# RWKV-7 stretches of a hybrid block: one DMA queue and the prices in a written-out order

## The chip, the cores and the metric

The kernel runs on one core of one Trainium2 chip. The metric is the device time of one execution in microseconds (us). The kernel before took 2974.73 us, the median of 3 runs (2971.03 to 2976.58).

The engines are called by their short names: PE (TensorE, matmuls), PEld (its weight loads), DVE (VectorE), ACT (ScalarE), POOL (GpSimd) and SP (SyncE, which only issues DMAs). Each has its own stream of instructions, laid down when the kernel is built; a DMA is issued by an instruction in the stream of SP or ACT, with its waits.

## The reference

Two layers over 256 context tokens and 256 latent tokens of width 1024, batch 1. Each layer normalises and modulates its input, projects it, runs three mixers in both directions over the sequence, merges them by gates, and ends in a SwiGLU block:

```
for layer in range(2):
    h   = modulate(rms_norm(x), ...)              # 1024 x 512 tokens
    p   = h @ w_in                                # all mixers' inputs and the merge gates
    ml  = chunkwise mLSTM(p)                      # 4 heads of 256
    lru = depthwise conv + RG-LRU(p)
    rw  = RWKV-7(p)                               # 16 heads of 64
    y   = sum_b sigmoid(g_b) * (b @ out_b);  x += gate * (y @ w_out)
    x  += gate * swiglu(modulate(rms_norm(x), ...))
```

RWKV-7 is the recurrence that the change is about. For each head and direction, with a 64 x 64 state S:

```
S_t = S_{t-1} (diag(w_t) - kap_t^T (a_t * kap_t)) + v_t^T k_t
y_t = S_t r_t
```

The latent tokens start from the final state of the context tokens. In the last layer the outputs for context tokens aren't needed. Everything is 32-bit: each large product is split into three passes (high by low, high by high, low by high) to keep its accuracy.

## The kernel before

**Layout.** Features lie on the 128 partitions, tokens on the free axis (T = 512: context 0 to 255, latent 256 to 511). A large product is one block of 128 output features: 8 blocks of the contraction x 3 passes = 24 matmuls of 512 columns (or of 256, where only latent tokens count) into one PSUM tile `mm`. Its weights are one DMA of 512 KB into a tile `wraw` (two buffers, line 390); in two halves ACT rounds them to `whi` and DVE takes the rest as `wlo` (lines 470 and 473).

**RWKV-7 in units.** The recurrence is computed in chunks of 32 tokens. A unit u (0 to 7) is four heads and one half of the tokens: even units context, odd ones latent. Each unit passes through:

- `rw_load` (line 929): loads of the projected k, r, v and of the decay weights (`ax`), issued by SP.
- `rw_prep` (line 662): decays, normalised keys, scaled rows, then the small matmuls whose masked results are `Am` (line 781). One generator goes through the eight units in order; the preparation of unit u also waits for the chain of unit u - 3.
- `rw_solve` (line 950): the triangular system of each chunk. SP writes the blocks of `Am` to DRAM (`sc1`), loads them transposed as `N` (line 957), POOL eliminates in 30 steps of two operations on i x w elements with w = 31 - i (lines 963 and 965) and sets the diagonal (line 967), SP stores N (line 970) and loads it back into `Am` (line 975).
- `rw_tok` (line 853): token-major copies of keys and values (`UV`, `bkT`).
- `rw_chain` (line 979): eight chunks one after the other, each with some five groups of small matmuls and the steps `xs` (line 1034, DVE), `UV` (lines 1061 and 1064, ACT and DVE) and the new state `Sn` (line 1081, DVE) between them.
- `rw_tail`: norm, gate and store.

**The order.** Inside a stretch the instructions of PE, SP, DVE, ACT and POOL are laid down in an order that `weave` (line 299) works out when the kernel is built. Every task is a generator: it emits instructions and says what they cost in planned ns (`took`, `at`, `op`) or what it waits for (`until`, `wait`). `weave` keeps a planned clock `now`; of the tasks that are ready it takes the first of a fixed list: low-rank inputs, loads, preparation, chains, gate, and last the large products (`fill`). The products come earlier than their place in the list by one rule (line 332): if the columns that planned matmuls put through PE in the last `TICK` = 3413 ns of planned time are fewer than `COLS[l]`, the products get the turn. They also run whenever nothing else is ready. `TICK` appears a second time: at the end of each such tick `slow` becomes 2.0 when the tick's columns were 3100 (`THR`) or fewer, and all planned PE times are doubled until the next tick (lines 322 to 324, 350).

**The products of a stretch** (`products`, line 460): 74 blocks, first the RWKV inputs for the four pairs of units, then mLSTM's and the LRU's, whose results go to DRAM (`mld`, `lrd`). The load for product n + 2 is issued in the middle of product n (line 500), always by SP.

**Waits of the plan**: `DMW` ahead of the load of N, `DML` behind it and again behind the store of N, `DMR` behind the load back into `Am`.

**After the stretch** come the mLSTM and LRU stage, the 24 merge-gate blocks (`mg`, with `wblk`, `wload`, `wraw`: lines 411 to 417; matmuls at line 425, casts at lines 382 and 383, stores at line 1289), the merge itself and the feed-forward block. These are outside the written-out order: the framework places them, also between a stretch's instructions where they fit. In layer 1 they have 256 columns.

Of the kernel before, what the change touches and what calls it, by code (L numbers as in the profile page):

```python
# [30 lines left out]
NCH = T // CH  # L31
DSC = math.exp(-0.5)
TICK = 3413.0
DML = 4000
COLS = [4800, 4800]
GDP = 1
ORD = [0, 0]
SL = 1000
SW = 230
THR = 3100  # L40
PW = 1700
HYS = 0
DMW = 4000
DMR = 5000
JW = 4
JD = 6
# [166 lines left out]
class KB:  # L213
# [85 lines left out]
    def weave(self, tasks, cols):  # L299

        live = [[g, 0.0, None, False, 0.0, None] for g in tasks]
        fill = live[-1]
        self.now, recent = 0.0, []
        self.free = {"V": 0.0, "S": 0.0, "G": 0.0}
        tick, slow, count, burst = TICK, 1.0, 0.0, False


        def can(c):
            return c is None or (c[1] not in self.locks if c[0] == "lock" else c in self.done)

        eng = mybir.EngineType
        with self.tc.manual_schedule(engines={eng.PE, eng.SP, eng.DVE, eng.Activation, eng.Pool}):
            i = None
            while live:
                if i is None:
                    ok = [x for x in live if can(x[2])]
                    ready = [x for x in ok if x[1] <= self.now]
                    if not ready:
                        self.now = min(x[1] for x in ok)
                        continue  # L320
                    i = ready[0]
                    while self.now > tick:
                        tick += TICK
                        slow, count = (1.0 if count > THR else 2.0), 0.0
                    while recent and recent[0][0] < self.now - TICK:
                        recent.pop(0)
                    light = [x for x in ready if x[3]]
                    if light:
                        i = light[0]
                    elif fill in ready:  # L330

                        if sum(c for _, c in recent) < cols + (HYS if burst else -HYS):
                            i = fill
                        burst = i is fill
                    i[3] = False
                    if i[2] and i[2][0] == "lock":
                        self.locks.add(i[2][1])
                        i[4] = self.now
                    elif i[2]:
                        i[4] = max(i[4], self.now)  # L340
                    i[2] = None
                self.since, self.by, i[5] = i[4], i[5], None
                try:
                    k, *v = next(i[0])
                except StopIteration:
                    live.remove(i)
                    i = None
                    continue
                if k == "pe":
                    self.now += v[0] * slow  # L350
                    count += v[1]
                    recent.append((self.now, v[1]))
                    i[4] = self.now + PED
                    if i is fill:
                        i = None
                    continue
                if k == "spawn":
                    live.insert(live.index(i) + 1, [v[0], 0.0, None, False, max(self.now, self.since), None])
                    continue
                if k == "aside":  # L360
                    live.insert(0, [v[0], 0.0, None, True, v[1], None])
                    continue
                if k == "wait":
                    i[1] = i[4] = max(self.now, self.since) + v[0]
                elif k == "at":
                    i[1] = i[4] = v[0]
                elif k == "on":

                    i[1], i[3] = v[0], True
                    i[4], i[5] = v[1:] if len(v) > 1 else (v[0], None)  # L370
                elif k == "lock":
                    i[2] = (k, v[0])
                else:
                    i[2] = v[0]
                i = None
# [18 lines left out]
        self.nraw = -1  # L394
        es.callback(lambda: setattr(self, "wx", None))

    def wraw(self, src, n=1024):
        raw = self.rawtile()
        self.nc.sync.dma_start(out=raw[:, 0:n], in_=src)
        return raw  # L400

    def wpart(self, raw, i, n=512, pool=None):
# [57 lines left out]
    def products(self, jobs, h):  # L460


        raw = [self.wraw(self.A["wA"][j[0]]) for j in jobs[:2]]
        w = {}
        self.stores = []

        def part(n, i, first=False):
            hi, lo = (self.pw.tile([128, 512], F32R, name=x, tag=x, bufs=3) for x in ("whi", "wlo"))
            x = raw[n][:, 512 * i:512 * i + 512]
            self.nc.scalar.copy(hi, x)  # L470
            if not first:
                yield self.at("S", 615)
            self.nc.vector.tensor_tensor(out=lo, in0=x, in1=hi.bitcast(F32), op=ALU.subtract)  # L473
            w[2 * n + i] = [x.rearrange("p (k c) -> p k c", c=128) for x in (hi, lo)]
            yield self.end("V", 760)
            self.done.add(("w", w_id, 2 * n + i))

        def evac(n, ps):
            store = yield from jobs[n][2](ps)
            if store:  # L480
                self.stores.append(store)
            self.done.add(("evac", w_id, n))

        w_id = len(self.done)
        for i in range(2):
            yield ("aside", part(0, i, True), 0.0)
        for n, (_, t0, take) in enumerate(jobs):
            if n > 1:
                yield ("until", ("evac", w_id, n - 2))
            ps = self.mm()  # L490
            for k in range(KC):
                if k % 4 == 0:
                    yield ("until", ("w", w_id, 2 * n + k // 4))
                for i, (x, y) in enumerate(((0, 1), (0, 0), (1, 0))):
                    self.mmul(ps[:, t0:], w[2 * n + k // 4][x][:, k % 4], h[y][:, k, t0:], start=k == 0 and i == 0, stop=k == KC - 1 and i == 2)
                    yield self.took(0.0)
                if k % 4 == 0 and n + 1 < len(jobs):
                    yield ("aside", part(n + 1, k // 4), 0.0)
                    if k == 4 and n + 2 < len(jobs):
                        raw.append(self.wraw(self.A["wA"][jobs[n + 2][0]]))  # L500
                if k == 3:
                    while self.stores:
                        self.stores.pop(0)()
            yield ("aside", evac(n, ps), self.now + PED)
        yield ("until", ("evac", w_id, len(jobs) - 1))
        while self.stores:
            self.stores.pop(0)()
# [442 lines left out]
    def rw_solve(self, l, u, Am, sc1):  # L950

        nc, G, re = self.nc, self.nc.gpsimd, self.re
        if u:
            yield ("until", ("solve", l, u - 1))
        yield ("wait", DMW)
        N = re.tile([64, 32, 32], F32, name="N")
        nc.sync.dma_start(out=N, in_=sc1.rearrange("x h q s t -> (x h q) s t"))
        yield ("wait", DML)
        et = re.tile([64, 256], F32, name="et")
        for i in range(1, 31):  # L960
            w = 31 - i
            tv = et[:, 0:i * w].rearrange("p (a b) -> p a b", b=w)
            G.tensor_tensor(out=tv, in0=N[:, 0:i, i:i + 1].broadcast_to([64, i, w]), in1=N[:, i:i + 1, i + 1:32].broadcast_to([64, i, w]), op=ALU.mult)  # L963
            yield ("on", self.op("G", 240 + 2.0 * i * w) - 1500)
            G.tensor_tensor(out=N[:, 0:i, i + 1:32], in0=N[:, 0:i, i + 1:32], in1=tv, op=ALU.subtract)  # L965
            yield ("on", self.op("G", 300 + 1.85 * i * w) - 1500)
        G.memset(N.rearrange("p s t -> p (s t)")[:, 0:1024:33], -1.0)
        yield ("on", self.op("G", 100) + LAT)
        sc2 = self.dr.tile([2, 2, 16, 32, 32], F32, name="sc2")
        nc.sync.dma_start(out=sc2.rearrange("x h q s t -> (x h q) s t"), in_=N)  # L970
        yield ("wait", DML)
        for hd in range(2):
            for j in range(2):
                b = 64 * hd + 32 - 32 * j
                nc.sync.dma_start(out=Am[b:b + 32, j, :, :, 0:32].rearrange("p d c t -> p (d c) t"), in_=sc2[hd, j].rearrange("q s t -> s q t"))
        self.ready[u] = max(self.now, self.since) + DMR
        self.done.add(("solve", l, u))
# [880 lines left out]
```

## Time and profile before

| | |
|---|---|
| median of 3 runs | 2974.73 us |
| the profiled execution | 2970.17 us |
| its span, first to last instruction | 2968.5 us |
| mean granted clock of PE | 0.955 |
| PE busy | 2648.7 us, 89% |
| PEld busy | 2039.5 us, 69% |
| DVE busy | 1761.2 us, 59% |
| ACT busy | 1264.0 us, 43% |
| POOL busy | 810.0 us, 27% |
| DMA | 421.04 MB, mean 142 GB/s |

PE's busy time is an upper estimate, since matmuls overlap and their ends are modelled. The granted clock is a share of full speed: the records know 1.00 (2.4 GHz) and 0.50 (1.2 GHz), and a mean between is a mix of the two. The stretch of layer 0 lies at about 50 to 850 us, that of layer 1 at about 1700 to 2500 us. "Idle before" a group is time in which its engine did nothing, put down to what ended the wait; on an engine that nobody waits for it costs nothing.

### The profile page before, as it was taken

Reading aid. Unit: us, or ns where it says so; the run is one execution under the profiler, and the core shown is the slowest. Engines: PE = TensorE matmul, PEld = TensorE weight load, DVE = VectorE, ACT = ScalarE, POOL = GpSimd, SP = SyncE. Lnnn points to the kernel's source line nnn. Section 1 sums busy time; section 2 is a strip of 40 time slices with the busy share of each in tenths; the row PEclk is TensorE's granted clock in tenths of the full one; section 3 lists DMA queues with packets and bytes.
Section 4 is the critical chain, followed back from the end, with each engine's and each line's share of the span. In section 5 each row is a group of like instructions: output and inputs, shape, how many; then the busy total and the mean of one; then the engine's idle time right before and its main releaser. Section 6 shows DMA issues by size and latency. Waiting matters only on the chain. (4 is left out here: it accounts for less than half of the span.)

```text
span 2968.5 us, 71161 instructions
## 1 busy us (share of the span) xinstructions
PE 2648.7 (89%) x29512; PEld 2039.5 (69%) x29512; DVE 1761.2 (59%) x3642; ACT 1264.0 (43%) x2495; POOL 810.0 (27%) x1231
## 2 busy tenths in 40 slices
PE   7998999999789999999999989899996765769998
PEld 4775666666555576777777878776775654349898
DVE  5575667666468844553333456667675646767664
ACT  4443433333247732342222455444443422755553
POOL 1045545455403100010000101564645550100000
PEclk9999999999899999999999999999997886879999
DMA  6443333433254277655554445444443333327454
GB/s 225 164 143 108 115 116 112 116 113 103 62 193 126 92 234 237 216 172 167 168 166 132 126 149 163 141 130 122 132 122 93 88 101 117 93 86 255 150 183 143
DMA packets 242307, 421.04 MB, mean 142 GB/s; under 512 B 86048, under 2 KB 133408, under 8 KB 241984
## 3 DMA queue, kind: packets, MB, share of 16 engines
q1 hardware_dynamic: 240688, 415.39, 45.2%
q8 instruction: 231, 3.78, 0.5%
q10 hardware_dynamic: 1296, 1.10, 0.1%
q14 instruction: 92, 0.75, 0.1%
HBM read 348.75 MB, written 66.62 MB: 140 GB/s over the span
## 5 line engine op out<-in xcount | busy, mean ns | idle before, releaser
L259 PE MATMUL mm<-hl,whi 128*128 128x512 f32 (+1 forms) x1184 | 451.4, 381 | 9.0 <-DVE stage L549 4.7
L259 PE MATMUL mm<-hh,wlo 128*128 128x512 f32 (+1 forms) x1184 | 451.5, 381 | 0.8 <-DVE wlo L473 0.8
L259 PE MATMUL mm<-hh,whi 128*128 128x512 f32 (+1 forms) x1184 | 450.2, 380 | 0.0
L383 DVE TENSOR_TENSOR wlo<-wraw,whi 128x512 fp32r<-128x512 f32 (+1 forms) x310 | 219.3, 709 | 292.7 <-ACT whi L382 289.5
L425 PE MATMUL mm<-hl,whi 128*128 128x512 f32 (+1 forms) x1056 | 372.4, 353 | 2.5 <-ACT fg L1763 1.9
L425 PE MATMUL mm<-hh,wlo 128*128 128x512 f32 (+1 forms) x1056 | 366.8, 348 | 4.5 <-DVE wlo L383 4.5
L382 ACT CAST whi<-wraw 128x512 fp32r<-128x512 f32 (+1 forms) x310 | 189.3, 614 | 419.6 <-PE mm L425 261.9
L425 PE MATMUL mm<-hh,whi 128*128 128x512 f32 (+1 forms) x1056 | 367.7, 348 | 0.0
L473 DVE TENSOR_TENSOR wlo<-wraw,whi 128x512 fp32r<-128x512 f32 x296 | 236.2, 799 | 150.4 <-ACT whi L470 149.5
L965 POOL TENSOR_TENSOR N<-N,et 64x30 f32<-64x30 f32 (+14 forms) x480 | 295.8, 616 | 37.5
L963 POOL TENSOR_TENSOR et<-N 64x30 f32<-64x30 f32 (+14 forms) x480 | 281.4, 586 | 54.2 <-DMA N<-sc 17.7
L1207 POOL TENSOR_TENSOR nsq<-nsq,stage 128x256 f32<-128x256 f32 (+1 forms) x28 | 26.3, 938 | 862.7 <-ACT stage L1205 663.2
L259 PEld LDWEIGHTS mm<-hl,whi 128*128 128x128 f32 x1184 | 225.3, 190 | 52.5 <-ACT whi L470 6.1
L259 PEld LDWEIGHTS mm<-hh,wlo 128*128 128x128 f32 x1184 | 225.3, 190 | 44.7 <-DVE wlo L473 3.2
L259 PEld LDWEIGHTS mm<-hh,whi 128*128 128x128 f32 x1184 | 225.1, 190 | 42.2 <-issue 1.8
L382 ACT CAST whi<-wx 128x512 fp32r<-128x512 f32 x212 | 128.8, 609 | 260.8 <-PE mm L425 162.2
L470 ACT CAST whi<-wraw 128x512 fp32r<-128x512 f32 x296 | 180.5, 616 | 132.7 <-DMA wraw<-in_wA_dram 63.6
L425 PEld LDWEIGHTS mm<-hl,whi 128*128 128x128 f32 x1056 | 203.7, 193 | 47.7 <-ACT whi L382 15.8
L383 DVE TENSOR_TENSOR wlo<-wx,whi 128x512 fp32r<-128x512 f32 x212 | 144.8, 683 | 145.0 <-ACT whi L382 140.1
L425 PEld LDWEIGHTS mm<-hh,wlo 128*128 128x128 f32 x1056 | 203.3, 192 | 35.5 <-DVE wlo L383 5.4
L425 PEld LDWEIGHTS mm<-hh,whi 128*128 128x128 f32 x1056 | 203.9, 193 | 23.4 <-issue 0.7
L1061 ACT COPY UV<-u 32x128 f32<-32x128 f32 x256 | 65.6, 256 | 341.0 <-DVE UV L1064 339.7
(321 smaller groups left out, 5383.4 us busy)
## 6 DMA issues: line engine op xcount, KB each, us to landing
wraw<-in_wA_dram SPq DMA_DIRECT2D x275, 512.0 KB, 3.8
wx<-in_wA_dram SPq DMA_DIRECT2D x81, 512.0 KB, 3.6
wx<-in_wM_dram SPq DMA_DIRECT2D x55, 512.0 KB, 9.0
wraw<-in_wM_dram SPq DMA_DIRECT2D x41, 512.0 KB, 4.2
mld<-stage SPq DMA_DIRECT2D x48, 256.0 KB, 2.5
wraw<-in_wB_dram SPq DMA_DIRECT2D x23, 512.0 KB, 3.5
pd<-stage SPq DMA_DIRECT2D x40, 256.0 KB, 2.2
ax<-in_aux_dram SPq DMA_DIRECT2D x32, 256.0 KB, 4.9
```

What stands on the lines that cost most here:

```text
L259: self.nc.tensor.matmul(out, lhsT, rhs, start=start, stop=stop)
L382: self.nc.scalar.copy(hi[i], x[i])
L383: self.nc.vector.tensor_tensor(out=lo[i], in0=x[i], in1=hi[i].bitcast(F32), op=ALU.subtract)
L425: self.nc.tensor.matmul(ps, x[k], y[:, koff + k, t0:t0 + n], start=start and i == 0, stop=stop and i == 3 * nk - 1)
L470: self.nc.scalar.copy(hi, x)
L473: self.nc.vector.tensor_tensor(out=lo, in0=x, in1=hi.bitcast(F32), op=ALU.subtract)
L963: G.tensor_tensor(out=tv, in0=N[:, 0:i, i:i + 1].broadcast_to([64, i, w]), in1=N[:, i:i + 1, i + 1:32].broadcast_to([64, i, w]), op=ALU.mult)
L965: G.tensor_tensor(out=N[:, 0:i, i + 1:32], in0=N[:, 0:i, i + 1:32], in1=tv, op=ALU.subtract)
L1061: SC.copy(UV[j][b, :, i], us[b, j])
L1207: (eng or self.nc.gpsimd).tensor_tensor(out=nsq, in0=nsq, in1=sq, op=ALU.add)
```

## The change

Five edits, all in the stretches:

- The planned price of a solve's step goes from 240 + 2.0 i w and 300 + 1.85 i w to 280 + 2.3 i w and 340 + 2.1 i w; `DMW` from 4000 to 5500 and `DML` from 4000 to 4500.
- `slow` and `THR` are gone: planned PE times are never doubled.
- `COLS` goes from 4800 to 3000 in both layers.
- `wraw` can issue on another engine, and the loads for products from the third on are issued by ACT.
- All other loads (the first two of a stretch, those of the merge gates and of all that follows) stay with SP.

Instructions and data of the arithmetic stay the same; their order in the five streams changes, since the planner's prices and rules do.

```diff
-DML = 4000
-COLS = [4800, 4800]
+DML = 4500
+COLS = [3000, 3000]
...
-THR = 3100
...
-DMW = 4000
+DMW = 5500
...
-        tick, slow, count, burst = TICK, 1.0, 0.0, False
+        tick, count, burst = TICK, 0.0, False
...
                     while self.now > tick:
                         tick += TICK
-                        slow, count = (1.0 if count > THR else 2.0), 0.0
+                        count = 0.0
...
                 if k == "pe":
-                    self.now += v[0] * slow
+                    self.now += v[0]
...
-    def wraw(self, src, n=1024):
+    def wraw(self, src, n=1024, eng=None):
         raw = self.rawtile()
-        self.nc.sync.dma_start(out=raw[:, 0:n], in_=src)
+        (eng or self.nc.sync).dma_start(out=raw[:, 0:n], in_=src)
...
                     if k == 4 and n + 2 < len(jobs):
-                        raw.append(self.wraw(self.A["wA"][jobs[n + 2][0]]))
+                        raw.append(self.wraw(self.A["wA"][jobs[n + 2][0]], eng=self.nc.scalar))
...
-            yield ("on", self.op("G", 240 + 2.0 * i * w) - 1500)
+            yield ("on", self.op("G", 280 + 2.3 * i * w) - 1500)
...
-            yield ("on", self.op("G", 300 + 1.85 * i * w) - 1500)
+            yield ("on", self.op("G", 340 + 2.1 * i * w) - 1500)
```

## Rows read from the trace of the kernel before

**Rows 1.** Page, sections 1 and 2: busy us; granted clock in 40 slices

```profile
PE 2648.7 (89%) x29512; PEld 2039.5 (69%) x29512; DVE 1761.2 (59%) x3642; ACT 1264.0 (43%) x2495; POOL 810.0 (27%) x1231
PEclk9999999999899999999999999999997886879999
```

**Rows 2.** Windows by stage: us, busy us per engine (instructions), clock, DMA share, GB/s

```profile
50.00:740.00 690.00, 641.74 (x9664) 476.45 (x9662) 451.70 (x936) 285.82 (x595) 307.36 (x455) 0.99 0.41 123
740.00:850.00 110.00, 90.98 (x1889) 63.41 (x1889) 50.47 (x129) 27.33 (x64) 39.28 (x68) 0.92 0.27 77
1700.00:2240.00 540.00, 500.59 (x7187) 402.74 (x7187) 353.29 (x707) 255.70 (x540) 237.69 (x347) 0.98 0.45 136
2240.00:2500.00 260.00, 169.85 (x3788) 140.77 (x3765) 141.71 (x339) 80.32 (x190) 109.26 (x178) 0.81 0.34 94
2500.00:2650.00 150.00, 103.32 (x370) 56.04 (x370) 112.25 (x259) 98.69 (x177) 19.40 (x47) 0.81 0.32 97
```

**Rows 3.** Windows, the same columns: the five places where TensorE stands still

```profile
231.00:246.00 15.00, 5.63 (x68) 4.03 (x66) 3.67 (x10) 1.21 (x2) 1.50 (x5) 0.76 0.53 141
2255.00:2277.00 22.00, 2.40 (x27) 1.98 (x26) 0.52 (x1) 1.17 (x3) 13.07 (x28) 0.58 0.24 72
2344.00:2355.00 11.00, 0.42 (x4) 0.22 (x2) 0.99 (x2) 2.24 (x7) 2.42 (x9) 0.69 0.56 121
2420.00:2441.00 21.00, 0.00 (x1) 0.00 (x0) 0.23 (x1) 0.37 (x1) 12.63 (x27) 0.58 0.27 56
777.00:793.00 16.00, 0.87 (x5) 0.33 (x3) 1.82 (x4) 0.90 (x2) 9.71 (x21) 0.64 0.23 48
```

**Rows 4.** Timeline, 2266 to 2278 us: start, us, what, [idle before, what ended it]

```profile
2270.14 0.46 SPq L970 DMA_DIRECT2D sc<-N  x1
2271.32 0.58 SPq L399 DMA_DIRECT2D wraw<-in_wA_dram  x1
2275.83 0.62 ACT L382 CAST whi<-wraw 128x512 fp32r<-128x512 f32 x1 [23.20 <-DMA wraw<-in_wA_dram]
2276.48 0.69 DVE L383 TENSOR_TENSOR wlo<-wraw,whi 128x512 fp32r<-128x512 f32 x1 [22.37 <-ACT whi L382]
2277.43 0.33 PE L259 MATMUL u<-xs,Am 32*32 32x64 f32 x4 [20.03 <-DVE xs L1034]
```

**Rows 5.** Waits of SP's queue, whole run: us in total, times, longest

```profile
SPq L970 <- POOL N L967: 187.7, 14, 25.6
SPq L399 <- DVE wlo L473: 22.9, 19, 5.4
```

**Rows 6.** Timeline of POOL: first and last instruction of one solve

```profile
2230.13 0.23 POOL L963 TENSOR_TENSOR et<-N 64x30 f32<-64x30 f32 x1
2269.97 0.15 POOL L967 MEMSET N<- 64x32 f32 x1
```

**Rows 7.** Windows of tile mm (product matmuls, their evictions); PE groups in 50:740

```profile
50.00:740.00 690.00, 472.99 (x1796) 323.55 (x1796) 37.25 (x50) 45.84 (x74) 0.99 0.41 123
1700.00:2240.00 540.00, 374.77 (x1819) 284.24 (x1817) 32.84 (x51) 38.79 (x74) 0.98 0.45 136
2240.00:2500.00 260.00, 96.01 (x566) 79.42 (x566) 0.00 (x0) 8.99 (x24) 0.81 0.34 94
...
L259 PE MATMUL mm<-hh,wlo 128*128 128x512 f32 x592 | 240.8, 407 | 0.0
```

**Rows 8.** Lines L781, L1034 by window: count, duration ns, first and last start us

```profile
L781 DVE TENSOR_TENSOR Am<-sm,cst x32: 414/550/692, 1826.3 to 2382.9; 128x256 f32<-128x256 f32 x16, 128x512 f32<-128x512 f32 x16
...
L1034 DVE COPY xs<-xy x8: 277/284/292, 560.2 to 626.4; 128x128 f32<-128x128 f32 x8
...
L1034 DVE COPY xs<-xy x8: 282/291/292, 788.8 to 828.7; 128x128 f32<-128x128 f32 x8
```

**Rows 9.** ACT's waits in 1700:2240; line L1840, an issue on ACT

```profile
ACT whi L470 <- DMA wraw<-in_wA_dram: 41.8, 21, 6.5
...
L1840 ACTq DMA_DIRECT2D out_dram<-y x4: 338/344/353, 2962.0 to 2965.5; - x4
```

## The prediction

> **What bounds the kernel now.** I read the page first. TensorE (PE) is busy for 89% of the span, and its granted clock is nearly full but for slices 33 to 36 of the 40, each 74 us long, where it falls to seven and eight tenths [rows 1]. So the kernel is mostly limited by TensorE, and time is to be had where TensorE has nothing to do or runs at a lower clock. The change touches only the two RWKV-7 stretches, so I then cut those out as windows [rows 2]: 50 to 740 us (layer 0, large products there), 740 to 850 (layer 0, large products used up), 1700 to 2240 and 2240 to 2500 (the same two parts of layer 1), and 2500 to 2650, the mLSTM stage after it. With large products TensorE is busy 93% of the time at clock 0.99 and 0.98. Without them it is busy 91 of 110 us at 0.92, and in layer 1 only 170 of 260 us at 0.81.
>
> Third, inside those windows, I looked for where TensorE stands still. Five places hold most of it [rows 3]: in 231 to 246 us TensorE works 5.6 of 15.0 us, then 2.4 of 22.0, 0.4 of 11.0, 0.0 of 21.0 and 0.9 of 16.0. That leaves 85.0 - 9.3 = 75.7 us with no matmul, all next to the end of a triangular solve on GpSimd (POOL).
>
> Fourth, the timeline of one of them shows the mechanism [rows 4]. At 2270.14 SyncE (SP) issues the store of the solved N (L970), and only 1.2 us later the merge gates' weight load behind it (L399). ACT's cast of `whi` ends a 23.2 us wait for such a load; VectorE's (DVE's) `wlo` ends a 22.4 us wait for the cast; the chain's `xs` stands behind it on DVE, and when it is done a 20.0 us wait of TensorE ends. SP had stood before L970 all that time. Over the run SP waits 187.7 us for the solve in front of L970, 14 times, up to 25.6 us [rows 5]. The order has the store too early: the planner prices a solve at 30 x (240 + 300) + (2.0 + 1.85) x 4960 = 35.3 us (4960 is the sum of i x w over its 30 steps), and the solve of unit 5 in layer 1 ran from 2230.13 to 2270.12, 40.0 us [rows 6].
>
> **The change part by part.** *Solve times.* The new prices give 30 x (280 + 340) + (2.3 + 2.1) x 4960 = 40.4 us, what the trace shows. With 1.5 us more ahead of the load of N and 0.5 us more behind it, L970 moves 7.1 us later in SP's order; with 0.5 us more behind the store, the chain starts 7.6 us later in the plan. At the first place of [rows 3] TensorE is parked in front of a chain whose solve is late, for 15.0 - 5.6 = 9.4 us. I take 7 us of this as regained; the bounds are 0 (the products ahead run dry instead) and 9.4.
>
> *Weights on ACT's queue.* Of 74 products in each layer, all but the first two loads move: 144 issues. The one issue on ACT in the trace that is like it, an output store, takes 0.34 us [rows 9], so ACT's sequencer gets 144 x 0.34 = 49 us of new work. ACT is busy 286 of 690 and 256 of 540 us in the two stretches [rows 2], so most of it lies in idle time; where it falls just ahead of a `UV` copy of the chain, it delays a step by 0.34 us. The load waits for its buffer, that is for DVE's `wlo`, and behind it on ACT stand the chain's `UV` copies and the casts of the next product: SP's 19 waits of this kind add up to 22.9 us [rows 5], and that is the upper bound for what ACT can inherit. Against it ACT itself now waits 41.8 us in layer 1 for weights [rows 9]. From -15 to +25 us; I take +3, nearest to issues that are hidden. The Trainium skill, page "DMA: Bandwidth & Descriptors", section "Issuing engines are not separate DMA queues", says that starting transfers from several engines only saves the sequencer's time for the issue. By that rule alone the move would be worth 49 us of SP's time, which nobody waits for, and the term would be 0 instead of +3; the trace differs from it in one thing, since what the loads wait for at the five places is neither the issue nor the transfer but an instruction ahead of them in SP's order [rows 4].
>
> *Large products less urgent.* The planner gives a ready product the turn while the columns of the last 3413 ns of its own plan are under the bound. In layer 0, 3 x 592 products of 512 columns in 690 us are 1318 columns per us, 4500 in 3413 ns [rows 7]: products sat just under the old bound of 4800 by themselves, so steps of the chain and of the preparation that were ready gave way time and again. With 3000 they give way only in dense bursts. A chain beside products took (626.4 - 560.2) / 7 = 9.5 us per chunk, the last chain of layer 0 beside few of them (828.7 - 788.8) / 7 = 5.7 us [rows 8]. But the units follow one another at the pace of the preparation: `Am` is masked from 1826.3 to 2382.9 us for eight units, some 79 us each [rows 8], and it goes no faster after 2240 us than before, so VectorE and latencies set most of it. I take 3 us for each of six units of layer 1, 18 us; bounds 0 and 6 x 8 = 48. In layer 0 TensorE is the limit and the pace by itself gives nothing.
>
> What it gives there is that products are left over for the end. At 777 to 793 us they would fill 15.1 us; I take 12. In layer 1 the places at 2255 (19.6 us idle) and 2344 (10.6) would come to lie where products still run, with weights that don't queue behind L970: I take 17 and 9. The last, 2420 to 2441 (21.0), is behind the last solve, where I expect few products: 8.
>
> *What is late next.* The merge gates' products, 566 matmuls of which stand in 2240 to 2500 [rows 7], are the filler of that window now, and they still load from SP. If half of the 24 move into the next stage, TensorE has room (103 of 150 us busy) but VectorE less (112 of 150) [rows 2]: two splits of some 0.7 us [rows 4] for each of twelve, 17 us; I take 15 (0 to 34). With fewer products between the small matmuls the clock can also fall. Nothing in the trace shows the bursts of the new order; the mean is 0.99 and 0.98 with the old one and 0.81 with few products, so I take 10 us (0 to the rival below).
>
> *No doubled TensorE time.* The order of before doubled TensorE's times after a planned tick with under 3100 columns. With products at 4500 that is rare, so it acts at the ends of the stretches only; with the new bound it would have acted often. Priced at nothing (-5 to +5).
>
> **The sum.** 7 + 12 + 17 + 9 + 8 + 18 = 71 us gained, 15 + 10 + 3 = 28 given back: 43 us. The profiled execution took 2970.17 us (its span is 2968.5, 1.7 us lie around it), so 2927; the median of the runs is 4.6 us above that execution, so I predict 2932 us.
>
> **The rivals.** *The stalls stay.* The products are used up before the last units again; the merge gates' loads still queue behind L970, which is only 7.1 us later. Then each of five places loses 7 us at most, no pace is won, and the clock and ACT take 13: -22 us, 2953. For it: SP waits of 20 to 25 us are longer than 7.1, and the loads at 2271 us are not moved to ACT [rows 4]. Against it: eight units need the same products spread over longer.
>
> *The clock falls: slower.* In bursts of small matmuls the order no longer puts products between, and TensorE drops from 2.4 to 1.2 GHz in the middle of the stretch; a product's matmul then takes twice as long. For it: between 2240 and 2500 us TensorE had few wide matmuls and the mean clock was 0.81, and at none of the five places was it over 0.76 [rows 2, 3]. Against it: products keep running wherever nothing else is ready. Products occupy 473 + 375 = 848 us of TensorE here [rows 7]. At a mean clock of 0.90 they cost 848 x (1/0.90 - 1/0.985) = 81 us more; with 71 - 18 = 53 us gained otherwise that is 2970 + 28 + 5 = 3003 us. It decides from a mean clock under 0.93, where 848 x (1/0.93 - 1/0.985) is 51 us. The Trainium skill, page "TensorE: Matmul & The Clock Gate", section "Part 1: The HAM clock gate", says the throttled state is the default and activity releases it; the rows just named agree, and no row shows the new bursts.
>
> *Nothing moves.* Preparation sets the pace by VectorE's order, layer 0 is bound by TensorE in any case, and waits come up in other places as fast as they go: 2970 to 2977 us.
>
> **How the numbers follow.** Forecast 0.50 (its own range 2900 to 2950), stalls stay 0.18, clock falls 0.21, nothing moves 0.08; 0.03 is for still more than forecast. From no measurement of this kernel can a change under 0.2%, 6 us, be told from none. Faster: 0.50 + 0.18 + 0.03 = 0.71, slower 0.21, same 0.08. The range is 2880 to 2992: down to the larger pace term with all idle places filled, up into most of the clock's case.
>
> **What would show it.** Right: in the changed profile the five empty places are gone but perhaps the last one, SP's wait for the solve at L970 is under 100 us in total, TensorE's products in layer 1 end after 2300 us, the last chain ends some 40 us sooner in layer 1, and the merge gates come later. Wrong: the products end at about the same time, or waits of 10 us and more for `wraw` remain on ACT, or ACT waits for `wlo` in front of a load by tens of us, or the clock of the stretches is under 0.95.

## The result: 1.26% faster, and the profile after

The changed kernel takes 2937.89 us (median of 4 runs, 2930.44 to 2940.11) against 2975.07 (4 runs, 2971.03 to 2976.58): a ratio of 0.9874, 95% interval 0.9858 to 0.9890. The forecast was 2932 us in 2880 to 2992. The profiled execution took 2936.28 us, span 2934.6, against 2970.17 and 2968.5. Behind the edits, lines stand two lower than before: the store of N is L968, the solve's end L965, the products' casts L468 and L471, the merge gates' casts L380 and L381.

First the page (busy us; granted clock in 40 slices) and the windows by stage, after, with the columns of [rows 2].

```profile
PE 2648.2 (90%) x29512; PEld 2042.8 (70%) x29512; DVE 1764.4 (60%) x3642; ACT 1266.3 (43%) x2495; POOL 811.2 (28%) x1231
PEclk9999999999999999999999999999999787879999
```

```profile
50.00:740.00 690.00, 633.85 (x10310) 471.21 (x10309) 458.47 (x955) 285.47 (x596) 328.96 (x497) 0.99 0.39 117
740.00:850.00 110.00, 102.47 (x1254) 72.66 (x1253) 64.00 (x159) 35.85 (x76) 17.53 (x36) 0.99 0.47 152
1700.00:2240.00 540.00, 492.99 (x7404) 396.59 (x7405) 363.21 (x729) 254.12 (x542) 260.80 (x381) 0.98 0.44 131
2240.00:2500.00 260.00, 190.05 (x3557) 153.46 (x3555) 149.60 (x356) 93.89 (x213) 92.33 (x156) 0.83 0.40 116
2500.00:2650.00 150.00, 106.85 (x462) 67.02 (x463) 113.12 (x245) 95.16 (x168) 16.98 (x37) 0.83 0.33 103
```

PE does the same work (2648.2 against 2648.7 us), and of the 33.9 us by which the span is shorter 33.4 were standing still. More of the RWKV matmuls now lie beside products: 10310 instructions instead of 9664 in the first window, in less busy time. The granted clock of the two windows with products is what it was, 0.99 and 0.98; in 740 to 850 us, where products now run too, it is 0.99 instead of 0.92.

Of the five empty places three are gone. These are the windows at the first and fifth place of [rows 3], and at the two that remain, later in layer 1 (same columns).

```profile
231.00:246.00 15.00, 13.26 (x365) 10.14 (x365) 6.83 (x13) 5.99 (x14) 4.21 (x2) 1.00 0.72 177
777.00:793.00 16.00, 15.83 (x414) 10.29 (x406) 8.70 (x25) 4.08 (x11) 0.00 (x0) 1.00 0.22 73
2303.00:2319.00 16.00, 2.03 (x38) 1.71 (x40) 1.33 (x4) 2.02 (x5) 7.67 (x19) 0.61 0.29 90
2381.00:2398.00 17.00, 2.02 (x26) 1.70 (x25) 1.39 (x4) 1.41 (x4) 8.62 (x21) 0.61 0.30 69
```

The 75.7 us of [rows 3] have become 1.7 + 0.2 + 14.0 + 15.0 = 30.9. The two that are left lie at the end of the solves of units 6 and 7, as the places at 2344 and 2420 did: the first has grown from 10.6 to 14.0 us, the second shrunk from 21.0 to 15.0. Both have the mechanism of [rows 4], step for step; the timeline around 2312 us (start, us, what, [idle before, what ended it]):

```profile
2312.07 0.45 SPq L968 DMA_DIRECT2D sc<-N  x1
2312.63 0.53 SPq L397 DMA_DIRECT2D wraw<-in_wA_dram  x1
...
2317.16 0.62 ACT L380 CAST whi<-wraw 128x512 fp32r<-128x512 f32 x1 [13.82 <-DMA wraw<-in_wA_dram]
2317.80 0.26 ACT L1059 COPY UV<-u 32x128 f32<-32x128 f32 x1
...
2318.11 0.71 PE L258 MATMUL u<-UV,bkT 64*64 64x64 f32 x16 [13.97 <-ACT UV L1059]
```

SP stood before the store of N; the weights of a merge gate were issued 0.56 us behind it; ACT waited for them with the chain's `UV` copy next in its stream, and PE waited for `UV`. Only the chain's step differs from [rows 4], `UV` on ACT instead of `xs` behind DVE. SP's waits over the run, against [rows 5] (us in total, times, longest):

```profile
SPq L968 <- POOL N L965: 74.3, 12, 22.9
...
SPq L397 <- DVE wlo L471: 12.4, 3, 6.0
```

Products (windows of tile `mm`, against [rows 7]; the first two stretched to where products now end), the masks and one chain (against [rows 8]: count, ns, first and last start), and ACT's wait for product weights in the stretch of layer 1 beside its new issues (against [rows 9]). In the last row of tile `mm` 576 of the 611 matmuls are the merge gates', all they have; the others are the end of the products.

```profile
50.00:770.00 720.00, 465.96 (x1777) 321.90 (x1778) 37.17 (x50) 45.87 (x74) 0.99 0.40 118
1690.00:2246.00 556.00, 368.39 (x1809) 283.23 (x1809) 32.89 (x51) 38.89 (x74) 0.98 0.45 133
2240.00:2500.00 260.00, 104.32 (x611) 86.59 (x609) 0.00 (x0) 9.94 (x26) 0.83 0.40 116
```

```profile
L779 DVE TENSOR_TENSOR Am<-sm,cst x32: 411/550/693, 1818.6 to 2343.0; 128x256 f32<-128x256 f32 x16, 128x512 f32<-128x512 f32 x16
...
L1032 DVE COPY xs<-xy x8: 277/280/292, 536.5 to 594.8; 128x128 f32<-128x128 f32 x8
```

```profile
ACT whi L468 <- DMA wraw<-in_wA_dram: 26.7, 24, 2.3
...
L397 ACTq DMA_DIRECT2D wraw<-in_wA_dram x144: 334/334/370, 53.4 to 2235.8; - x144
```

The eight units of layer 1 pass the mask in 524.4 us instead of 556.6; a chain beside products takes 58.3 / 7 = 8.3 us per chunk instead of 9.5. The last chain of layer 0 ends at 805 instead of 829 us, that of layer 1 at 2442 instead of 2478, the mLSTM stage of layer 1 begins 33 us sooner, and the 34 us last to the end.

### The profile page after: what moved, and what is told of

Same layout as the page of the kernel before. It is cut to its first block, busy times and chain, and to the rows that moved or that the text cites. A ratio compares the mean times of both kernels' runs of the same rounds, so it can differ in the third digit from the quotient of the medians.

```text
span 2934.6 us, 70988 instructions
## 1 busy us (share of the span) xinstructions
PE 2648.2 (90%) x29512; PEld 2042.8 (70%) x29512; DVE 1764.4 (60%) x3642; ACT 1266.3 (43%) x2495; POOL 811.2 (28%) x1231
## 5 line engine op out<-in xcount | busy, mean ns | idle before, releaser
L381 DVE TENSOR_TENSOR wlo<-wraw,whi 128x512 fp32r<-128x512 f32 (+1 forms) x310 | 214.7, 694 | 270.5 <-ACT whi L380 266.8
L380 ACT CAST whi<-wraw 128x512 fp32r<-128x512 f32 (+1 forms) x310 | 189.6, 614 | 371.2 <-PE mm L423 243.7
L961 POOL TENSOR_TENSOR et<-N 64x30 f32<-64x30 f32 (+14 forms) x480 | 288.3, 601 | 56.4 <-DMA N<-sc 20.1
L963 POOL TENSOR_TENSOR N<-N,et 64x30 f32<-64x30 f32 (+14 forms) x480 | 289.5, 603 | 37.4
L471 DVE TENSOR_TENSOR wlo<-wraw,whi 128x512 fp32r<-128x512 f32 x296 | 232.7, 787 | 104.4 <-ACT whi L468 100.0
L258 PEld LDWEIGHTS mm<-hh,whi 128*128 128x128 f32 x1184 | 224.7, 190 | 42.8 <-issue 1.2
L380 ACT CAST whi<-wx 128x512 fp32r<-128x512 f32 x212 | 128.7, 608 | 264.5 <-PE mm L423 164.7
L381 DVE TENSOR_TENSOR wlo<-wx,whi 128x512 fp32r<-128x512 f32 x212 | 144.7, 683 | 147.8 <-ACT whi L380 141.7
L468 ACT CAST whi<-wraw 128x512 fp32r<-128x512 f32 x296 | 181.3, 617 | 113.9 <-PE mm L258 71.5
L1519 PE MATMUL mm<-ylo,whi 128*128 128x256 f32 (+1 forms) x544 | 186.4, 343 | 19.5 <-DVE ylo L381 19.3
```

Of the source, the lines that this page charges most:

```text
L258: self.nc.tensor.matmul(out, lhsT, rhs, start=start, stop=stop)
L380: self.nc.scalar.copy(hi[i], x[i])
L381: self.nc.vector.tensor_tensor(out=lo[i], in0=x[i], in1=hi[i].bitcast(F32), op=ALU.subtract)
L1519: self.nc.tensor.matmul(ps, x[k], y[k][:, t0:t1], start=i == 0, stop=i == 3 * KC - 1)
```

## The experiments

The theory is the prediction's: weights queue in SP's order behind a store that comes too early, and the right solve prices, the second queue and the later products free them. The rivals are that one edit does it all, that the two rules of the planner (bound and doubling) do nothing or harm, and that the clock pays for the later products. **S** stands for the solve times with `DMW` and `DML`, **A** for the loads issued by ACT, **C** for `COLS` 3000, **D** for no doubled PE times. All ratios are to the kernel before, run on the same chip, with a 95% interval; each changed kernel has 4 to 12 runs, the kernel before 4 to 23 on each chip. The two waits are SP's in front of the store of N over the run, and ACT's for product weights in 50 to 850 plus 1700 to 2300 us.

| kernel | us | ratio (95%) | SP's wait | ACT's wait |
|---|---|---|---|---|
| before | 2975.07 | 1 | 187.7 | 63.5 |
| S | 2958.06 | 0.9946 (0.9933-0.9959) | 132.6 | 51.3 |
| A | 2966.83 | 0.9974 (0.9961-0.9987) | 190.2 | 32.2 |
| C | 3129.32 | 1.0515 (1.0501-1.0530) | 334.2 | 106.6 |
| D | 2980.16 | 1.0019 (1.0005-1.0034) | 160.9 | 64.1 |
| C, D | 2984.69 | 1.0030 (1.0017-1.0043) | 157.0 | 100.6 |
| A, C, D | 2958.62 | 0.9940 (0.9922-0.9959) | 156.2 | 38.6 |
| S, C, D | 2952.07 | 0.9924 (0.9908-0.9941) | 66.1 | 56.2 |
| S, A, D | 2952.89 | 0.9922 (0.9905-0.9938) | 63.6 | 42.8 |
| S, A, C, D (after) | 2937.89 | 0.9874 (0.9858-0.9890) | 74.3 | 33.7 |

### One part alone

**S.** The edit is the `DML`, `DMW` and price lines of the diff.

```diff
-DML = 4000
+DML = 4500
-DMW = 4000
+DMW = 5500
-            yield ("on", self.op("G", 240 + 2.0 * i * w) - 1500)
+            yield ("on", self.op("G", 280 + 2.3 * i * w) - 1500)
...
```

> The solve prices and the three waits alone (DMW 5500, DML 4500, 280 + 2.3 i w, 340 + 2.1 i w), everything else as before. My theory: this is the edit that takes away TensorE's park in front of chains whose solve is late (9.4 us in layer 0, 5.3 us in layer 1) and shortens SP's waits at the store of N from 187.7 to under 110 us, but the merge gates' loads stay behind that store in the last units; 12 to 25 us faster, ratio 0.992 to 0.996. Rival (the planner's prices only shuffle waits; the bound on columns or the queue does the work): ratio 0.998 to 1.003.

0.9946, 16 us: right prices by themselves give a share, and SP's wait goes down by 55 us to 132.6, not under the 110 expected. PE's empty place at 231 us is gone, and the 15.1 us of the one at 777 are 5.9. In layer 1 PE's three longest waits up to the end of the last chain, 20.0, 10.6 and 21.1 us before, are 13.8, 7.1 and 20.6.

**A.**

```diff
-                        raw.append(self.wraw(self.A["wA"][jobs[n + 2][0]]))
+                        raw.append(self.wraw(self.A["wA"][jobs[n + 2][0]], eng=self.nc.scalar))
```

> The products' weights on ACT's queue alone. My theory: 49 us of issue time on ACT, hidden, and loads that no longer queue behind the store of N in the stretch with products; ratio 0.998 to 1.003, ACT's 41.8 us of waits for weights in layer 1 become under 25. Rival (the queue is what frees the stretch): ratio under 0.994.

0.9974, 8 us faster, a little more than expected. SP's wait is as long as before, but the product weights no longer stand behind it: ACT waits 32.2 us for them instead of 63.5 (26.3 of them in layer 1, not quite under 25). So the term of +3 us had the wrong sign. Of PE's empty places only the one at 231 us goes; the others keep 14.9, 21.4, 10.5 and 21.3 us, since the merge gates' loads are still SP's.

**C**, with the doubling left in.

```diff
-COLS = [4800, 4800]
+COLS = [3000, 3000]
```

> The bound on columns alone, 3000 in place of 4800, with the doubled TensorE time kept. My theory: preparations and chains go faster and products are left for the ends; the idle 15 us in layer 0's tail shrinks; ratio 0.992 to 0.998. Rival (the clock falls in bursts): ratio over 1.002 and mean clock of 50 to 740 us under 0.97. Second rival (VectorE sets the pace): 0.998 to 1.002 with the same interval from Am to Am.

1.0515: 153 us slower, the largest effect of the study. SP's wait (columns as above), the windows by stage, and the windows of tile `mm` over this kernel's products:

```profile
SPq L970 <- POOL N L967: 334.2, 16, 34.7
```

```profile
50.00:740.00 690.00, 579.33 (x8749) 423.43 (x8747) 390.95 (x832) 253.91 (x525) 267.48 (x411) 0.92 0.35 104
1700.00:2240.00 540.00, 461.42 (x5162) 373.96 (x5160) 292.65 (x592) 219.38 (x448) 185.33 (x275) 0.92 0.39 118
...
50.00:910.00 860.00, 502.84 (x1777) 327.27 (x1778) 37.23 (x50) 45.94 (x74) 0.92 0.33 99
1838.00:2569.00 731.00, 408.74 (x1787) 297.74 (x1788) 32.38 (x50) 38.87 (x74) 0.88 0.36 105
```

PE is short of work in both stretches (579 busy us of 690, before 642), and all 16 solves now keep SP waiting, up to 34.7 us. The granted clock is 0.92 in both stretches, 0.99 and 0.98 before. So both signs of the rival named for this run, that the clock falls in bursts, came true (a ratio over 1.002, a clock under 0.97). The products' matmuls keep PE busy for 503 and 409 us; over the products of the kernel before (50 to 727 and 1722 to 2239 us) it is 468 and 370. Over the run PE is busy for 2714.6 us instead of 2648.7 with the same instructions. So the lower clock costs some 66 to 74 of the 153 us, an estimate from these rows, and standing still the rest.

The plan suggests why. The rule stops pushing products at 3000 columns, and a tick with 3100 or fewer doubles the next tick's PE times: in the order of before 46 of 236 planned ticks of layer 0 are doubled, in this one 250 of 339 (layer 1: 78 of 219 and 163 of 259; counted in the plan, no time of the chip). The solve's prices are not doubled with them, so the order has PE far slower than it is, next to solves that look short.

**D.**

```diff
-                        slow, count = (1.0 if count > THR else 2.0), 0.0
+                        count = 0.0
-                    self.now += v[0] * slow
+                    self.now += v[0]
```

> Only the doubling of planned TensorE time is removed. My theory: with the old bound a planned tick seldom has under 3100 columns while products last, so the order changes at the ends alone; ratio 0.998 to 1.002. Rival (planned time after the products' end is doubled all along, which is where the order was wrong): ratio under 0.996.

1.0019, barely clear of 1: some 5 us slower by itself. With the old bound the doubling was of a little use. The same three waits shrink to 6.4, 10.2 and 14.3 us and the time doesn't, so the empty places are not the whole account.

### Pairs and all but one

**C and D** together: the lines of the two diffs above.

```diff
-COLS = [4800, 4800]
+COLS = [3000, 3000]
-                    self.now += v[0] * slow
+                    self.now += v[0]
```

> The bound of 3000 together with the removal of the doubling; solve prices, waits and queue as before. The bound alone made 1.0515, with SP's waits at the store of N at 334 us against 188. Theory (the doubling turned the low bound into a plan twice as slow as the chip; without it the bound gives the preparation and the chains a faster pace): 0.993 to 0.998. Rival (a low bound is harmful in itself, and the whole change is fast because of solve prices and queue, -0.5% and -0.3%): over 1.000.

1.0030. D takes back all but 0.3% of the 5.15%, so that in this change the two are one edit; but the pair by itself gains nothing: the theory's 0.993 to 0.998 did not come, the rival's "over 1.000" did. The windows by stage, and ACT's waits for product weights (us, times, longest), 50 to 850 and 1700 to 2300 us of this kernel:

```profile
50.00:740.00 690.00, 623.88 (x9661) 467.26 (x9659) 444.09 (x922) 277.54 (x576) 314.67 (x457) 0.96 0.39 114
...
1700.00:2240.00 540.00, 475.60 (x6639) 387.09 (x6637) 346.68 (x695) 240.71 (x512) 232.16 (x334) 0.97 0.43 127
```

```profile
ACT whi L469 <- DMA wraw<-in_wA_dram: 46.0, 19, 8.9
...
ACT whi L469 <- DMA wraw<-in_wA_dram: 54.6, 21, 7.3
```

The waits are longer than before (21.7 and 41.8), and the granted clock is lower, 0.96 and 0.97.

**All but S** is the whole change with the old prices:

```diff
-DMW = 5500
+DMW = 4000
-            yield ("on", self.op("G", 280 + 2.3 * i * w) - 1500)
+            yield ("on", self.op("G", 240 + 2.0 * i * w) - 1500)
...
```

> The whole change but with the old solve prices and waits. Theory (the parts add up; solve prices are worth 0.5%): 0.991 to 0.995. Rival (with the low bound and no doubling the plan runs ahead of the chip at every solve, so the prices are worth more than alone): over 0.996, SP's waits at the store of N over 180 us.

**All but A** has every load on SP again:

```diff
-                        raw.append(self.wraw(self.A["wA"][jobs[n + 2][0]], eng=self.nc.scalar))
+                        raw.append(self.wraw(self.A["wA"][jobs[n + 2][0]]))
```

> The whole change but with all weights on SP. Theory (the queue is worth 0.26% alone and the same here): 0.989 to 0.992. Rival (with SP no longer held at the store of N the queue has nothing left to give): 0.986 to 0.988.

**All but C** has the old bound:

```diff
-COLS = [3000, 3000]
+COLS = [4800, 4800]
```

> The whole change but with the bound left at 4800. Theory (the bound is worth some 0.5% by the pace of the units and the products left for layer 0's tail): 0.991 to 0.995. Rival (solve prices and queue make all of it): 0.986 to 0.989, and the products of layer 0 end later than 729 us all the same.

0.9940, 0.9924 and 0.9922. Against 0.9874 each of the three is worth about half a per cent within the whole: S 0.66, A 0.50, C 0.48, each give or take some 0.24. A is worth more than alone, against both readings that stood ahead of its run. The low bound that gained nothing by itself pays once prices and queue are right: S, A and the pair C, D multiplied give 0.9946 x 0.9974 x 1.003 = 0.9950, the whole 0.9874; 0.76%, give or take 0.28, some 23 us, is there only together. The two waits move with it: with the pair alone ACT waits 100.6 us for weights, 38.6 with A added, 56.2 with S added, 33.7 with both. So no single edit does it, and the bound is not idle. What the doubling costs is shown beside the old prices alone (C against C, D); the whole without D alone was not run.

The kernel without C says something more. Its products end at 705 and 2222 us, sooner than before, and yet one place alone is left of the five, 19.9 us at the end of unit 7's solve (a new one, at 735 us, has 5.4). The solves of units 5 and 6 end at 2285 and 2355 us, and SP waits 3.4 and 2.6 us for them (25.6 and 20.3 before). So the other four need no later products: the prices, the queue and D free them. Where C's half per cent lies is open. What the traces show is that the granted clock of 2240 to 2500 us is 0.77 without C and 0.83 with it, and that of 740 to 850 us 0.97 and 0.99.

### How low the bound may be

```diff
-COLS = [3000, 3000]
+COLS = [1500, 1500]
```

> The changed kernel with a bound of 1500 in place of 3000 in both layers. Theory (VectorE sets the pace of the units by now, so a lower bound wins no pace, and the small matmuls stand alone for longer): 0.987 to 0.993, the clock of 50 to 750 us under 0.98. Rival (the lower the bound the more products are left for layer 1's end): 0.980 to 0.985, products of layer 1 ending after 2270 us.

2938.84 us, ratio 0.9871 (0.9856 to 0.9885): the same as the change. The granted clock is 0.97 in 50 to 750 and in 1700 to 2240 us (in the slowest of the five runs, 2955.69 us, which is the profiled one). That is under 0.98, as the theory had it, and lower than the change's 0.99 and 0.98; but the products' matmuls keep PE busy for 462 and 365 us, in the change for 466 and 365, so the lower clock did not reach them.

### The two places that are left

If the merge gates' loads behind the store of N are their cause, they should go when these loads leave SP. First all 48 such loads, issued by ACT:

```diff
-                            K.gemm(ps[:, t0:], K.wblk(l, f"mg{b}_{j}"), h, t0, T - t0)
+                            K.gemm(ps[:, t0:], K.wblk(l, f"mg{b}_{j}", nc.scalar), h, t0, T - t0)
```

> The changed kernel, and besides the 48 merge-gate loads are issued by ACT in place of SP. Theory (the two places left in layer 1 where TensorE stands still, 14.0 and 15.0 us, are there because these loads stand behind the store of N in SP's order): both are gone or under 5 us, SP still waits 20 us at that store twice, ratio to before 0.978 to 0.983. Rival (the stream of ACT is held in their place, by loads that wait for a buffer, or TensorE waits for the chain anyway): 0.986 to 0.990, with new waits of ACT.

2947.27 us, 0.9908 (0.9891 to 0.9925): a third of a per cent slower than the change, and the two places keep 8.2 and 12.6 us. The timeline of this kernel around 2400 us:

```profile
2399.76 0.45 SPq L969 DMA_DIRECT2D sc<-N  x1
2400.31 0.53 SPq L1288 DMA_DIRECT2D mgd<-stage  x1
...
2403.34 0.38 ACT L1287 ACTIVATE stage<-mm 128x256 f32<-128x256 f32 x1 [15.63 <-DMA mgd<-stage]
...
2403.78 0.58 PE L424 MATMUL mm<-hl,whi 128*128 128x256 f32 x1 [12.61 <-ACT stage L1287]
```

The next thing in SP's queue is the store of a gate's result. Until it is out, ACT has no free `stage`, and PE no free `mm`. The same wait has found other cargo. Why this kernel is slower than the change, with smaller places, was not followed up. So then loads and stores of the merge gates, layer 1 only:

```diff
-            return lambda: self.nc.sync.dma_start(out=out[:, t0:], in_=x[:, t0:])
+            return lambda: (eng or self.nc.sync).dma_start(out=out[:, t0:], in_=x[:, t0:])
...
+                            K.gemm(ps[:, t0:], K.wblk(l, f"mg{b}_{j}", nc.scalar if last else None), h, t0, T - t0)
+                            K.spill_now(t0, mgd[:, b, j], AF.Tanh, 0.5, nc.scalar if last else None)(ps)()
```

> The changed kernel, and in layer 1 both the loads and the stores of the merge gates are issued by ACT. With the loads alone on ACT the two empty places kept 8.2 and 12.6 us, ACT now waiting for a staging buffer whose store stood behind SP's store of N. Theory (whatever of the gates stands behind the store of N holds ACT, then the chain, then TensorE): both places under 4 us, ratio 0.979 to 0.986. Rival (the chain of the last units has to wait for its solve in any case, and work done in the empty places is missing later, in the mLSTM stage): the places shrink, and the ratio stays at 0.986 to 0.991.

2919.6 us, on a chip where the kernel before takes 2968.59: 0.9842 (0.9829 to 0.9856), faster than both kernels. SP's wait, and the windows at the first place and over the stretch's end:

```profile
SPq L969 <- POOL N L966: 121.8, 12, 48.0
```

```profile
2303.00:2319.00 16.00, 14.46 (x235) 12.02 (x235) 12.09 (x32) 8.60 (x20) 10.76 (x20) 1.00 0.35 108
...
2240.00:2500.00 260.00, 200.99 (x3624) 159.80 (x3623) 164.38 (x388) 106.94 (x233) 96.91 (x163) 0.86 0.42 125
```

SP waits longer than in the change, 48.0 us at once at the first place, and PE is busy for 41.9 of the 49 us in 2267 to 2316: nothing stands behind that wait that PE needs. Over 2240 to 2500 us PE is busy 201 instead of 190 us; the last chain ends at 2429 instead of 2442. Of the two places one of 11.3 us is left, not under the 4 expected, at the end of SP's second wait, of 40.1 us:

```profile
2377.03 0.45 SPq L969 DMA_DIRECT2D sc<-N  x1
2379.95 1.90 SPq L974 DMA_DIRECT2D Am<-sc  x4
2382.11 0.34 ACTq L398 DMA_DIRECT2D wraw<-in_wA_dram  x1
...
2383.15 0.62 ACT L381 CAST whi<-wraw 128x512 fp32r<-128x512 f32 x1 [14.23 <-issue]
...
2383.82 0.58 PE L424 MATMUL mm<-hl,whi 128*128 128x256 f32 x1 [11.31 <-ACT whi L381]
```

ACT stands for 13 us in front of its own weight load at 2382.11, and the cast that PE waits for stands behind it. The profile names nothing that ended this wait. In the trace the load waits for the semaphore that the first load of `Am` behind the store of N raises, and that one landed at 2382.03. So SP's wait still seems to reach ACT there, by a semaphore that both queues use; no run tests it.

The last run takes the waiting instruction away instead of the cargo: POOL, which makes N, issues its store and the four loads back.

```diff
-        nc.sync.dma_start(out=sc2.rearrange("x h q s t -> (x h q) s t"), in_=N)
+        G.dma_start(out=sc2.rearrange("x h q s t -> (x h q) s t"), in_=N)
...
-                nc.sync.dma_start(out=Am[b:b + 32, j, :, :, 0:32]...
+                G.dma_start(out=Am[b:b + 32, j, :, :, 0:32]...
```

> The changed kernel with the store of N and the four loads back into Am issued by POOL, right behind its own elimination, in place of SP. Theory (SP's place in front of that store is what stalls): SP waits for POOL at no store of N, both empty places of layer 1 are under 4 us, ratio 0.979 to 0.986 less what POOL's issues take. Rival (issues and the wait for the store to land on POOL delay the next solve and the chain by several us per unit): ratio 0.988 to 1.000, solve to chain over 12 us.

2938.0 us, on the chip of the run above: 0.9895 (0.9881 to 0.9908), no faster than the change and in the rival's range. SP never waits for the solve, and the 14.0 us at 2303 to 2319 shrink to 4.7, the 15.0 at 2381 to 2398 to 1.5. But POOL now waits for its own store before it may load back (line, count, busy us and mean ns, idle before and what ended it):

```profile
L974 POOL DMA_DIRECT2D Am<-sc x64 | 42.2, 667 | 52.9 <-DMA sc<-N 39.4 <-DMA mld<-stage 5.1 <-issue 4.4
```

and PE has a new wait of 12.6 us for chain 7's `Am` at 2411. That these POOL times are what the rest of the gain went into is argued from the trace, not shown by a further run.

## Why the prediction came out, step by step

- **The mechanism of the queue was right, but not for all five places.** Orders in SP's queue behind an early store were a cause: S alone shortens the wait and the time, A alone takes cargo from behind it and shortens the time, and the runs on the gates move or remove the remaining places by moving what stands behind. I had read it off one place and written it of five. At 777 and 2420 us what ended PE's wait was the landing of the chain's own `Am`, in the kernel before:

```profile
792.54 0.39 PE L259 MATMUL u<-xs,Am 32*32 32x64 f32 x2 [15.13 <-DMA Am<-sc]
...
2441.11 0.39 PE L259 MATMUL u<-xs,Am 32*32 32x64 f32 x2 [21.10 <-DMA Am<-sc]
```

  There a chain waits for its own solve, and PE has nothing else to do; at 2420 us a gate's weights stand behind the store as well.
- **Places in layer 1: too much, and by the wrong road.** 17 + 9 + 8 = 34 us were expected of 51.2 idle; 51.2 became 29.0, so 22 came, 19.6 from unit 5, -3.4 from unit 6 and 6.0 from unit 7. I took products to last to the end of the stretch; they end at 2246 instead of 2239 us, relative to an 11 us earlier start some 18 us later, and not after 2300. That stood in my list as a sign of being wrong. The last units run beside merge gates as before, with weights from SP. This is the rival "the stalls stay" in two places of five. And the kernel without C frees the places of units 5 and 6 with no later products at all.
- **Pace: same time counted twice.** Six times 3 us were expected; the units follow one another at 74.4 instead of 79.0 us, 32 us over layer 1. But the places at 2255 and 2344 lie within that pace. From the first preparation to the end of the last chain layer 1 won 24.5 us (708.2 to 683.7), where 34 + 18 = 52 stood in the sum.
- **Layer 0: 7 + 12 = 19 us;** its two places gave 7.7 + 14.9, and its last chain ends 24 us sooner. S alone, with products that end at 715 us instead of 726, already gives 9.2 of the 14.9 that I put down to later products. The merge of layer 0 starts only 14 us sooner: the merge gates' matmuls now run from 770 to 1062 us instead of 726 to 1076, and in both kernels the merge starts as they end. So the products left for the end of the stretch push the gates back there.
- **Given back: 25 us expected, none seen in the places named.** The merge gates of layer 1 did not move into the next stage: all 576 of their matmuls stand in 2240 to 2500 us, 566 before, and from the first matmul of the mLSTM stage to the first of the merge it takes 142 us in both kernels. The clock term of 10 was not paid: 0.99, 0.98 and 0.83 against 0.99, 0.98 and 0.81. That the clock can fall was no idle rival, though: it did with the bound of 3000 and the doubling (0.92), and a little with the pair C, D (0.96 and 0.97); with S and A beside the pair it did not. One reading was off, with no term resting on it: in [rows 1] the clock lies under nine tenths in slices 31 to 36, down to six tenths, where I read 33 to 36.
- **ACT's queue: the failed sign.** I took +3 us in -15 to +25; A gives -8 alone and -15 within the whole. The 144 issues are 144 x 0.334 = 48 us on ACT, as worked out from [rows 9], and no wait over 1 us stands in front of one of them: the loads' buffers are free when their turn comes. What I left out of the value, though I named it beside it, was ACT's own wait for weights. The Trainium skill's rule, on the page "DMA: Bandwidth & Descriptors", section "Issuing engines are not separate DMA queues", that issuing from several engines saves only the sequencer's time to start a transfer, would make this term 0. The runs differ from it: what is saved here is the time that an issue stands behind a waiting one.
- **The doubling: right at nothing, for a reason half right.** D alone is some +5 us, the end of the stated bounds. "That is rare" was wrong for the old order (a fifth of the planned ticks of layer 0, a third in layer 1); "with the new bound it would have acted often" was right, and its price, some 145 us between C and C with D, was worth a sentence of its own.
- **The sum:** 71 us of gains stood against 28 given back. The stages won 14 us (layer 0, to its merge) and 24.5 (layer 1's stretch), ACT's share within them, and some 4 were lost behind. Gains were put too large by some 33 us and losses by some 24, so the total, 34 us between the profiled executions against 43 forecast, is better than its terms: that the two errors have nearly cancelled is luck.

## What to carry to other kernels

A queue that issues in order makes its first waiting instruction everybody's wait: look at what stands behind a wait, not at how long it is. A wait of 48 us left PE no empty place once nothing urgent stood behind it, and one of 23 us left 14. When idle places and a pace are both to be won, check that they are not the same microseconds. And rules of a planner that work on the same quantity (here the columns of a tick) are one edit: half of this one is 5% slower.

## What I had not expected

- Issue times: 334 ns for a weight load on ACT, 667 ns for a load back of `Am` on POOL.
- The granted clock of the two product stretches: 0.99 and 0.98 before and in the change, 0.97 with its bound at 1500, 0.96 and 0.97 with C and D alone, 0.92 with C alone.
- The edits gain more together than one by one, 0.76% of the time. That what one frees the others use is my reading of the two waits, not shown by a run of its own.
